# A chunked scan in pairs of 64-token chunks, and the old states' products in four column groups

## The chip, the cores and the metric

The kernel runs on one core of one Trainium2 chip. The metric is the device time of one launch in microseconds (us), median of three runs. The core's engines are TensorE (PE in the profile; PEld is its weight load), VectorE (DVE), ScalarE (ACT), GpSimd (POOL) and SyncE (SP), which issues the loads of the weights.

## The reference

One layer of a decoder with width 2048 is applied to a prompt of 256 tokens, with 16 learned meta tokens ahead of it, and to a sample group of 8 sequences of 4 tokens, which carry old states. All is float32. The input is normalised and projected. Half of the mixing width goes to eight heads of a gated linear recurrence, the other half to a short convolution. An output projection, a norm, a SwiGLU feed-forward part and a second norm follow. The change touches the recurrence alone:

```python
def step(S, inp):                       # one chunk of c tokens, per head
    qc, kc, vc, gc = inp
    b = jnp.cumsum(gc, axis=2)          # log of the decay since the chunk's start
    b_mid = b[:, :, mid:mid + 1]
    b_last = b[:, :, -1:]
    a = jnp.einsum('bhtk,bhsk->bhts', qc * jnp.exp(b - b_mid), kc * jnp.exp(b_mid - b))
    a = jnp.where(causal, a, 0.0)
    o = (jnp.einsum('bhts,bhsv->bhtv', a, vc)
         + jnp.einsum('bhtk,bhkv->bhtv', qc * jnp.exp(b), S))
    S = (jnp.exp(b_last[:, :, 0, :, None]) * S
         + jnp.einsum('bhsk,bhsv->bhkv', kc * jnp.exp(b_last - b), vc))
    return S, o
```

For the prompt the meta tokens are one chunk of 16 and the 256 tokens four chunks of 64. For the samples each sequence is one chunk of 4 tokens, and its S is the old state of that sequence and head, a matrix of 128 by 128. Results are the outputs of both groups, the new states and the convolution's last inputs.

## The kernel before, in words

Everything is kept feature-major: 128 features on the partitions, the 304 tokens (16 meta, 256 prompt, 32 sample) along the row. The weights come as a stream of pieces of 512 KB, each split into a high and a low part, `hi` (ScalarE, L72) and `lo` (VectorE, L73). A *job* (`run_job`, L161 on) makes two output blocks of 128 features from 16 blocks of input: for each input block six wide products, `hi` by the input's high part (L176), `hi` by its low part (L177), `lo` by its high part (L178). So a job of the input projection has 96 wide products. The order of the jobs is fixed by `ORDER`: four jobs for each pair of heads (`zb` the forget gate, `vb` the values, `qb`, `gb`), three for each pair of convolution blocks (`cb`, `xb`, `gbb`), 28 in all, and then those of `wo`, the output projection, 8 of them, and the feed-forward part.

Other work is written as generators that are laid beside the jobs. After each six wide products `tick()` lets every lane of generators go on by one step; `yield n` skips n such steps. The lane `scan` holds `scan_head`, one generator per head, one head after the other. A scheduler sets the order on each engine from there; each engine then works its list off in that order, and waits where an operand is not there.

A head (`scan_head`, L467 on) goes through these steps, each line a step or two of the lane. The bank names are those of the profile; each bank is 512 columns of f32 in PSUM, and four are cycled for this work (the wide products have four others).

- `vtb` (L480 to L482): transposes of the values to token-major: the two chunk pairs of the prompt, the samples, the meta tokens; `vsb` (L495): the sample values once more, four times over in high and low parts.
- On ScalarE and VectorE: the log forget gates, their running sums `b` (L521, started anew at each chunk), decays `eb`, `el` (L525 to L537), the queries and keys with decay `eq`, `ek`, `qe` (L550 to L554). GpSimd multiplies the old states by their decay, `sn` (L548).
- `ktb` (L559 to L561): transposes of the decayed keys; `ab` (L566, L567): keys by queries. Two prompt products of 128 tokens each hold two chunks; a mask (`cmask`, L576) keeps the causal part inside each chunk and writes it into `at_b`. The samples' 32 by 32 product goes through `smask` into `ats_b` (L577).
- `kv` (L583, L584): each chunk's addition to the state, from the 64 rows of that chunk; the two halves of a 128-row tile write to two banks. The meta tokens' is a product of 16 rows.
- `sb` (L587, L588): the samples' additions to all eight states. VectorE then makes the states ahead of chunks 0 to 3 (`sts`, L591, L595) and the last one (`sfin`), and adds `sb` to `sn` (L599, L601).
- `ob`: the outputs. For the prompt `at_b` by the values (L608), and for each chunk the state ahead of it by its queries, 64 columns each (L609). After one more step the samples: `ats_b` by the values (L611), and eight products of an old state by the four queries of its sequence (L614).
- `nb` (L621): the mean square of the outputs; then the norm, the gate and the split into `mh`, `ml`, which `wo` reads.

An f32 product stands in the profile as two instructions (two passes), each with its own weight load; the products of split operands and the transposes are one.

Of the kernel before, what the change touches and what calls it, by code (L numbers as in the profile page):

```python
# [45 lines left out]
class InOrder:  # L46
    """An engine whose instructions keep the order in which they are written."""
# [10 lines left out]
def hybrid_step(ctx: ExitStack, tc: tile.TileContext, io):  # L58
# [102 lines left out]
    def run_job(rhs, n, name):  # L161
        """Next job of the stream: two output blocks of 128 features, [P, n] each."""
        first, ks = jobs[state["job"]]
        nk = len(ks)
        state["job"] += 1
        banks = [bank(f"{name}{m}", "main") for m in range(2)]
        for i, k in enumerate(ks):
            p = first + i // KB
            if i % KB == 0:
                ensure(p)  # L170
            hi, lo = splits[p]
            xh, xl = rhs(k)
            for m in range(2):
                cs = slice(m * P, (m + 1) * P)
                o = banks[m][:, :n]
                nc.tensor.matmul(o, hi[:, i % KB, cs], xh, start=(i == 0), stop=False)  # L176
                nc.tensor.matmul(o, hi[:, i % KB, cs], xl, start=False, stop=False)  # L177
                nc.tensor.matmul(o, lo[:, i % KB, cs], xh, start=False, stop=(i == nk - 1))  # L178
            tick()
        for p in range(first, first + (nk + KB - 1) // KB):  # L180
            del splits[p]
        return banks

# [30 lines left out]
    smask = const.tile([NS, DB, DS], F32, name="smask")  # L214
# [6 lines left out]
    ats_b = const.tile([NS, DB, DS], F32, name="ats_b")  # L221
# [6 lines left out]
    def make_constants():  # L228
        nc.gpsimd.memset(cmask, 1.0)
        nc.gpsimd.affine_select(out=cmask, in_=cmask, compare_op=ALU.is_ge, fill=0.0, base=0,  # L230
                                pattern=[[0, NPR], [1, P]], channel_multiplier=-1)
        nc.gpsimd.memset(cmask[:CH, :, CH:], 0.0)
        nc.gpsimd.memset(smask, 1.0)
        nc.gpsimd.affine_select(out=smask, in_=smask, compare_op=ALU.is_ge, fill=0.0, base=0,
                                pattern=[[DS, DB], [1, DS]], channel_multiplier=-1)
        nc.gpsimd.affine_select(out=smask, in_=smask, compare_op=ALU.is_ge, fill=0.0, base=0,
                                pattern=[[-DS, DB], [0, DS]], channel_multiplier=1)
# [40 lines left out]
    def newton(r, v, t):  # L278
        """One step towards r = v ** -0.5."""
# [5 lines left out]
    def rstd_tok(pool, mv, n, w, tag):  # L285
        """mv [., w, 2] mean and variance per row -> 1/sqrt(variance + eps), -mean/sqrt(variance + eps)."""
# [17 lines left out]
    with tc.tile_pool(name="x0", bufs=1) as x0p, tc.tile_pool(name="x0w", bufs=3) as x0w:  # L304
# [29 lines left out]
        def rstd(i):  # L334
            """1/sqrt(variance + eps) and -mean/sqrt(variance + eps) of each row."""
# [39 lines left out]
        def settle(k):  # L375
            """Block k of the normalised input, feature-major."""
# [76 lines left out]
    sp = s2.enter_context(tc.tile_pool(name="sp", bufs=1))  # L453

# [6 lines left out]
    def sview(t, o=NMETA + SEQ):  # L461
        return t[:, o : o + NS].rearrange("p (c t) -> p c t", t=DS)
# [3 lines left out]

    def scan_head(h, j, zs, vs, qs, gs):  # L467
# [9 lines left out]
        # values, token-major; log forget gate, key  # L477
# [3 lines left out]
        nc.tensor.transpose(vtb[:NS, 2 * P : 3 * P], vT[:, NMETA + SEQ :], ident)  # L481
# [20 lines left out]
        vts = sp.tile([NS, P], F32, tag="vts", name="vts")  # L502
        nc.scalar.copy(out=vts, in_=vtb[:NS, 2 * P : 3 * P])
        vtm = sp.tile([NMETA, P], F32, tag="vtm", name="vtm")
        nc.scalar.copy(out=vtm, in_=vtb[:NMETA, 3 * P :])
# [8 lines left out]
        nc.scalar.activation(out=w2, in_=w2, func=AF.Ln, bias=1.0)  # L514
        yield 1
# [7 lines left out]
        # decay factors  # L523
# [11 lines left out]
        nc.vector.tensor_tensor(out=sview(tm, SEQ), in0=bs, in1=bs[:, :, DS // 2 : DS // 2 + 1].broadcast_to([P, DB, DS]), op=ALU.subtract)  # L535
        yield 1
        nc.vector.tensor_mul(out=el, in0=kk, in1=el)  # L537
# [13 lines left out]
        nc.vector.tensor_mul(out=ek, in0=kk[:, NMETA:], in1=ek)  # L551
        yield 1
        qe = tl("qe", L)
        nc.vector.tensor_mul(out=qe, in0=q, in1=eb)  # L554
        yield 1
        # decayed keys, token-major; products within chunks
        ktb = bank("ktb")
        for c in range(NPR):
            nc.tensor.transpose(ktb[:, c * P : (c + 1) * P], el[:, NMETA + c * P : NMETA + (c + 1) * P], ident)  # L559
        nc.tensor.transpose(ktb[:, 2 * P : 3 * P], kd4.rearrange("p a b -> p (a b)").bitcast(F32), ident)  # L560
        nc.tensor.transpose(ktb[:NMETA, 3 * P :], el[:, :NMETA], ident)  # L561
        yield 1
# [4 lines left out]
        nc.tensor.matmul(ab[:NS, SEQ:L], ek[:, SEQ:], eq[:, SEQ:], start=True, stop=True)  # L567
        yield 3
# [4 lines left out]
        kdm = sp.tile([NMETA, P], F32, tag="kdm", name="kdm")  # L573
        nc.scalar.copy(out=kdm, in_=ktb[:NMETA, 3 * P :])
        yield 1
        nc.vector.copy_predicated(out=at_b, mask=cmask.bitcast(I32), data=ab[:, :SEQ].rearrange("p (a b) -> p a b", b=P))  # L576
        nc.vector.copy_predicated(out=ats_b, mask=smask.bitcast(I32), data=ab[:NS, SEQ:L].rearrange("p (a b) -> p a b", b=DS))  # L577
        yield 1
        # each chunk's addition to the state
        kv = [bank("kv0"), bank("kv1")]  # L580
        for c in range(NCH):
            ts = slice(c % 2 * CH, c % 2 * CH + CH)
            nc.tensor.matmul(kv[c % 2][:, c // 2 * P : c // 2 * P + P], kdt[ts, c // 2], vt[ts, c // 2], start=True, stop=True)  # L583
        nc.tensor.matmul(kv[0][:, 2 * P : 3 * P], kdm, vtm, start=True, stop=True)  # L584
# [5 lines left out]
        sts = sp.tile([P, NCH, P], F32, tag="sts", name="sts")  # L590
        nc.vector.tensor_copy(out=sts[:, 0], in_=kv[0][:, 2 * P : 3 * P])  # L591
        sfin = sp.tile([P, P], F32, tag="sfin", name="sfin", bufs=2)
        for c in range(NCH):
            dst = sts[:, c + 1] if c < NCH - 1 else sfin
            nc.vector.scalar_tensor_tensor(out=dst, in0=sts[:, c], scalar=eb[:, c * CH + CH - 1 : c * CH + CH],  # L595
                                           in1=kv[c % 2][:, c // 2 * P : c // 2 * P + P], op0=ALU.mult, op1=ALU.add)
# [8 lines left out]
        for c in range(NCH):  # L605
            cs = slice(c * CH, (c + 1) * CH)
            if c % 2 == 0:
                nc.tensor.matmul(ob[:, c * CH : c * CH + P], vt[:, c // 2], at_b[:, c // 2], start=True, stop=False)  # L608
            nc.tensor.matmul(ob[:, cs], sts[:, c], qe[:, cs], start=False, stop=(c % 2 == 1))  # L609
        yield 1  # L610
        nc.tensor.matmul(ob[:, SEQ:L], vts, ats_b.rearrange("p a b -> p (a b)"), start=True, stop=False)  # L611
        for bb in range(DB):
            cs = slice(SEQ + bb * DS, SEQ + (bb + 1) * DS)
            nc.tensor.matmul(ob[:, cs], s0[:, bb], qe[:, cs], start=False, stop=(bb == DB - 1))  # L614
        yield LAG
        # norm over the value width, output gate
# [221 lines left out]
    def normed(bk, t, u):  # L838
        """t = the product of the normalised input, but for u[:, 1] = its bias' part."""
# [139 lines left out]
    def shared(i, c):  # L979
        """Chunk c of tile i on ScalarE and GpSimd."""  # L980
# [13 lines left out]
    def whole(i, c):  # L994
        """Chunk c of tile i on VectorE."""
# [5 lines left out]
    def packed():  # L1001
        """The last tokens' scale, and their chunk on VectorE."""
# [52 lines left out]
```

## Time and profile before

| What | Before |
|---|---|
| median of three runs | 1451.89 us |
| lowest and highest | 1451.75, 1455.24 us |
| profiled execution: first to last instruction | 1451.5 us |
| profiled execution: its own device time | not listed apart |
| mean granted clock of TensorE | 0.986 |
| instructions | 25280, of which 10389 products |
| HBM traffic over the span | 159 GB/s |

The scan's products run from 88 us (first `vtb`) to 453 us (last `nb`). The page lists busy time, share of the span and number for each engine; in its second part each digit is one fortieth of the span, the row PEclk being the clock that TensorE was granted, in tenths. In rows of groups the two numbers behind the bar are the busy time in us and the mean in ns. The busy time of a product covers its way through the array, in which the next ones already run; what a product costs is read from the distance of the starts.

### The profile page before, as it was taken

Reading aid. Unit: us, or ns where it says so; the run is one execution under the profiler, and the core shown is the slowest. Engines: PE = TensorE matmul, PEld = TensorE weight load, DVE = VectorE, ACT = ScalarE, POOL = GpSimd, SP = SyncE. Lnnn points to the kernel's source line nnn. Section 1 sums busy time; section 2 is a strip of 40 time slices with the busy share of each in tenths; the row PEclk is TensorE's granted clock in tenths of the full one; section 3 lists DMA queues with packets and bytes.
Section 4 is the critical chain, followed back from the end, with each engine's and each line's share of the span. In section 5 each row is a group of like instructions: output and inputs, shape, how many; then the busy total and the mean of one; then the engine's idle time right before and its main releaser. Section 6 shows DMA issues by size and latency. Waiting matters only on the chain.

```text
span 1451.5 us, 25280 instructions
## 1 busy us (share of the span) xinstructions
PE 1405.6 (97%) x10389; PEld 1389.5 (96%) x10389; DVE 880.1 (61%) x1526; ACT 591.9 (41%) x824; POOL 128.1 (9%) x165
## 2 busy tenths in 40 slices
PE   5999999999999999999999999999999999999993
PEld 4999999999999999999999999999999999999992
DVE  6756675776576778965565554444555656544444
ACT  5644534544443444433343333333333343343331
POOL 5201111121010233000000000000000000020002
PEclk9999999999999999999999999999999999999997
DMA  6645545544544555455555545555555555575521
GB/s 188 211 153 163 161 148 162 162 145 147 171 136 147 158 165 160 148 171 162 161 167 167 161 151 169 160 170 178 160 168 166 160 164 162 169 231 160 161 89 65
DMA packets 221065, 232.14 MB, mean 160 GB/s; under 512 B 7655, under 2 KB 216659, under 8 KB 220629
## 3 DMA queue, kind: packets, MB, share of 16 engines
q1 hardware_dynamic: 217556, 218.80, 47.9%
q0 software_dynamic: 3392, 11.72, 2.8%
q8 instruction: 81, 1.33, 0.4%
q14 instruction: 36, 0.29, 0.1%
HBM read 223.34 MB, written 7.15 MB: 159 GB/s over the span
## 4 chain that ended last, share of the span: by engine, by line
PE 95%; DVE 3%; DMA 0%; ACT 0%; issue 0%; POOL 0%; SPq 0%; ACTq 0%; DVEq 0%
PE u L176 7%; PE u L178 6%; PE u L177 6%; PE wd L178 6%; PE g L176 6%; PE wd L177 6%; PE g L178 6%; PE g L177 6%; PE wd L176 6%; PE wo L178 2%; PE wo L177 2%; PE wo L176 2%; PE zb L176 1%; PE vb L176 1%; PE zb L177 1%; PE gbb L176 1%
## 5 line engine op out<-in xcount | busy, mean ns | idle before, releaser
L73 DVE TENSOR_TENSOR lo<-raw,hi 128x1024 fp32r<-128x1024 f32 (+1 forms) x408 | 498.9, 1224 | 466.4 <-ACT hi L72 466.0
L72 ACT CAST hi<-raw 128x1024 fp32r<-128x1024 f32 (+1 forms) x408 | 420.5, 1031 | 648.0 <-PE wd L177 146.2
L176 PE MATMUL g<-ygh,hi 128*128 128x290 f32 x704 | 209.8, 298 | 0.0
L178 PE MATMUL g<-ygh,lo 128*128 128x290 f32 x704 | 209.3, 297 | 0.0
L177 PE MATMUL g<-ygl,hi 128*128 128x290 f32 x704 | 209.1, 297 | 0.0
L176 PE MATMUL u<-ygh,hi 128*128 128x290 f32 x704 | 208.8, 297 | 0.0
L178 PE MATMUL u<-ygh,lo 128*128 128x290 f32 x704 | 208.7, 296 | 0.0
L177 PE MATMUL u<-ygl,hi 128*128 128x290 f32 x704 | 208.5, 296 | 0.0
L178 PE MATMUL wd<-ah,lo 128*128 128x288 f32 x704 | 207.9, 295 | 0.0
L177 PE MATMUL wd<-al,hi 128*128 128x288 f32 x704 | 207.9, 295 | 0.0
L176 PE MATMUL wd<-ah,hi 128*128 128x288 f32 x704 | 207.7, 295 | 0.0
L177 PEld LDWEIGHTS g<-ygl,hi 128*128 128x128 f32 x704 | 133.9, 190 | 0.1
L178 PEld LDWEIGHTS g<-ygh,lo 128*128 128x128 f32 x704 | 133.7, 190 | 0.0
L176 PEld LDWEIGHTS g<-ygh,hi 128*128 128x128 f32 x704 | 133.6, 190 | 0.1
L177 PEld LDWEIGHTS u<-ygl,hi 128*128 128x128 f32 x704 | 133.2, 189 | 0.0
L178 PEld LDWEIGHTS u<-ygh,lo 128*128 128x128 f32 x704 | 133.2, 189 | 0.0
L176 PEld LDWEIGHTS u<-ygh,hi 128*128 128x128 f32 x704 | 133.0, 189 | 0.0
L177 PEld LDWEIGHTS wd<-al,hi 128*128 128x128 f32 x704 | 132.3, 188 | 0.0
L176 PEld LDWEIGHTS wd<-ah,hi 128*128 128x128 f32 x704 | 132.2, 188 | 0.1
L178 PEld LDWEIGHTS wd<-ah,lo 128*128 128x128 f32 x704 | 132.2, 188 | 0.0
L178 PE MATMUL wo<-mh,lo 128*128 128x288 f32 x256 | 75.8, 296 | 0.0
L177 PE MATMUL wo<-ml,hi 128*128 128x288 f32 x256 | 75.6, 295 | 0.0
(337 smaller groups left out, 2525.8 us busy)
## 6 DMA issues: line engine op xcount, KB each, us to landing
raw<-in_w_in SPq DMA_DIRECT2D x112, 512.0 KB, 3.5
raw<-in_w_gate SPq DMA_DIRECT2D x88, 512.0 KB, 3.4
raw<-in_w_up SPq DMA_DIRECT2D x88, 512.0 KB, 3.4
raw<-in_w_down SPq DMA_DIRECT2D x80, 512.0 KB, 3.5
raw<-in_w_o SPq DMA_DIRECT2D x32, 512.0 KB, 3.5
s<-in_state_hgrn POOLq DMA_DIRECT2D x8, 512.0 KB, 4.8
out<-sn POOLq DMA_DIRECT2D x8, 512.0 KB, 4.1
raw<-in_w_down SPq DMA_DIRECT2D x16, 256.0 KB, 2.8
```

The source lines that it names most:

```text
L72: a.copy(out=hi, in_=src)
L73: v.tensor_tensor(out=lo, in0=src, in1=hi.bitcast(F32), op=ALU.subtract)
L176: nc.tensor.matmul(o, hi[:, i % KB, cs], xh, start=(i == 0), stop=False)
L177: nc.tensor.matmul(o, hi[:, i % KB, cs], xl, start=False, stop=False)
L178: nc.tensor.matmul(o, lo[:, i % KB, cs], xh, start=False, stop=(i == nk - 1))
```

## The change

The prompt is scanned in two pairs of chunks instead of four chunks. For a pair, `kp` holds the keys with decay to their own chunk's end, and those of the first chunk once more with the decay over the second; `qp` holds the queries with decay from their chunk's start, for the second chunk also from the pair's start. `ktb` transposes keys with decay to the pair's end, so that `kv` is one product of 128 rows per pair, in one bank; `ep` is the decay over a pair, and VectorE makes two states instead of four. What the second chunk of a pair takes from the first one is an own product, keys of the first by queries of the second (`ab`, two products of 64 columns), and is copied into the upper right quarter of `at_b`. Each pair's output is then one product of 128 columns with the state ahead of the pair.

The meta tokens' operands `kdm` and `vtm` are zeroed tiles of 128 rows, of which 16 are written. The samples' values come from `vsb`, on 128 rows (high parts on rows 0 to 31 and 64 to 95, low parts on the others); the samples' keys stand four times (`ek4`), and `smask` keeps the rows 0 to 63, so that high and low parts add up.

The eight products of the old states become four, `so`: the 32 queries of all sequences are the weights, two old states side by side are moved (256 columns), and each product writes its own 32 partitions of one bank. VectorE picks from the two halves the rows that belong to the sequence (`pmask`, one column for each half) and adds them (`os`), and a product with `fold` adds the four groups of 32 rows and turns them to feature-major, into `ob`. The constants `pmask` and `fold` are made by GpSimd at the start. Of the steps, there are now three ahead of `ktb` instead of one, two ahead of `ab`, two ahead of `so` and one behind it, one behind `os`, and the one between the parts of `ob` is gone.

```diff
-    smask = const.tile([NS, DB, DS], F32, name="smask")
+    smask = const.tile([P, DB, DS], F32, name="smask")
+    pmask = const.tile([P, 2], F32, name="pmask")
+    fold = const.tile([P, NS], F32, name="fold")
...
+    kdm = sp.tile([P, P], F32, name="kdm")
+    vtm = sp.tile([P, P], F32, name="vtm")
+    nc.gpsimd.memset(kdm, 0.0)
+    nc.gpsimd.memset(vtm, 0.0)
...
-        nc.tensor.transpose(vtb[:NS, 2 * P : 3 * P], vT[:, NMETA + SEQ :], ident)
...
-        vts = sp.tile([NS, P], F32, tag="vts", name="vts")
-        nc.scalar.copy(out=vts, in_=vtb[:NS, 2 * P : 3 * P])
+        vts = sp.tile([P, P], F32, tag="vts", name="vts")
+        nc.scalar.copy(out=vts, in_=vsb[:, :P])
...
+        ends = pairs(eb[:, :SEQ])[:, :, :, CH - 1 : CH]
         yield 1
-        nc.vector.tensor_mul(out=el, in0=kk, in1=el)
+        kp = sp.tile([P, NPR, 3, CH], F32, tag="kp", name="kp")
+        nc.vector.tensor_mul(out=kp[:, :, 0::2], in0=pairs(kk[:, NMETA : NMETA + SEQ]), in1=pairs(el[:, NMETA : NMETA + SEQ]))
+        nc.vector.tensor_mul(out=el[:, NMETA + SEQ :], in0=kk[:, NMETA + SEQ :], in1=el[:, NMETA + SEQ :])
+        nc.vector.tensor_mul(out=el[:, :NMETA], in0=kk[:, :NMETA], in1=el[:, :NMETA])
+        nc.vector.tensor_tensor(out=kp[:, :, 1], in0=kp[:, :, 0], in1=ends[:, :, 1].broadcast_to([P, NPR, CH]), op=ALU.mult)
...
-        nc.vector.tensor_mul(out=ek, in0=kk[:, NMETA:], in1=ek)
-        yield 1
-        qe = tl("qe", L)
-        nc.vector.tensor_mul(out=qe, in0=q, in1=eb)
-        yield 1
+        nc.vector.tensor_mul(out=ek[:, :SEQ], in0=kk[:, NMETA : NMETA + SEQ], in1=ek[:, :SEQ])
+        ek4 = sp.tile([P, P // NS, NS], F32, tag="ek4", name="ek4")
+        nc.vector.tensor_tensor(out=ek4, in0=kk[:, NMETA + SEQ :].unsqueeze(1).broadcast_to([P, P // NS, NS]),
+                                in1=ek[:, SEQ:].unsqueeze(1).broadcast_to([P, P // NS, NS]), op=ALU.mult)
+        yield 1
+        qp = sp.tile([P, NPR, 3, CH], F32, tag="qp", name="qp")
+        nc.vector.tensor_mul(out=qp[:, :, 0::2], in0=pairs(q[:, :SEQ]), in1=pairs(eb[:, :SEQ]))
+        qe = sp.tile([P, NS], F32, tag="qe", name="qe")
+        nc.vector.tensor_mul(out=qe, in0=q[:, SEQ:], in1=eb[:, SEQ:])
+        nc.vector.tensor_tensor(out=qp[:, :, 1], in0=qp[:, :, 2], in1=ends[:, :, 0].broadcast_to([P, NPR, CH]), op=ALU.mult)
+        ep = sp.tile([P, NPR, 1], F32, tag="ep", name="ep")
+        nc.vector.tensor_mul(out=ep, in0=ends[:, :, 0], in1=ends[:, :, 1])
+        yield 3
...
-        nc.tensor.matmul(ab[:NS, SEQ:L], ek[:, SEQ:], eq[:, SEQ:], start=True, stop=True)
-        yield 3
+        nc.tensor.matmul(ab[:, SEQ:L], ek4.rearrange("p a b -> p (a b)"), eq[:, SEQ:], start=True, stop=True)
+        xs = slice(SEQ + CH, SEQ + CH + NPR * CH)
+        for c in range(NPR):
+            nc.tensor.matmul(ab[:, xs][:, c * CH : (c + 1) * CH], kp[:, c, 0:2].rearrange("p a b -> p (a b)"), qp[:, c, 2], start=True, stop=True)
+        yield 2
+        so = bank("so")
+        for g in range(P // NS):
+            nc.tensor.matmul(so[g * NS : (g + 1) * NS, : 2 * P], qe, s0[:, 2 * g : 2 * g + 2].rearrange("p a b -> p (a b)"),
+                             start=True, stop=True)
+        yield 1
...
+        nc.vector.tensor_copy(out=at_b[:CH, :, CH:], in_=ab[:CH, xs].rearrange("p (a b) -> p a b", b=CH))
+        nc.vector.copy_predicated(out=ats_b, mask=smask.bitcast(I32), data=ab[:, SEQ:L].rearrange("p (a b) -> p a b", b=DS))
+        yield 1
+        os_ = sp.tile([P, P], F32, tag="os", name="os")
+        nc.vector.tensor_scalar(out=os_, in0=so[:, :P], scalar1=pmask[:, 0:1], scalar2=None, op0=ALU.mult)
+        nc.vector.scalar_tensor_tensor(out=os_, in0=so[:, P : 2 * P], scalar=pmask[:, 1:2], in1=os_, op0=ALU.mult, op1=ALU.add)
         yield 1
-        kv = [bank("kv0"), bank("kv1")]
-        for c in range(NCH):
-            ts = slice(c % 2 * CH, c % 2 * CH + CH)
-            nc.tensor.matmul(kv[c % 2][:, c // 2 * P : c // 2 * P + P], kdt[ts, c // 2], vt[ts, c // 2], start=True, stop=True)
-        nc.tensor.matmul(kv[0][:, 2 * P : 3 * P], kdm, vtm, start=True, stop=True)
+        kv = bank("kv")
+        for c in range(NPR):
+            nc.tensor.matmul(kv[:, c * P : (c + 1) * P], kdt[:, c], vt[:, c], start=True, stop=True)
+        nc.tensor.matmul(kv[:, 2 * P : 3 * P], kdm, vtm, start=True, stop=True)
...
-        for c in range(NCH):
-            cs = slice(c * CH, (c + 1) * CH)
-            if c % 2 == 0:
-                nc.tensor.matmul(ob[:, c * CH : c * CH + P], vt[:, c // 2], at_b[:, c // 2], start=True, stop=False)
-            nc.tensor.matmul(ob[:, cs], sts[:, c], qe[:, cs], start=False, stop=(c % 2 == 1))
-        yield 1
+        for c in range(NPR):
+            cs = slice(c * P, (c + 1) * P)
+            nc.tensor.matmul(ob[:, cs], vt[:, c], at_b[:, c], start=True, stop=False)
+            nc.tensor.matmul(ob[:, cs], sts[:, c], qp[:, c, 0:2].rearrange("p a b -> p (a b)"), start=False, stop=True)
         nc.tensor.matmul(ob[:, SEQ:L], vts, ats_b.rearrange("p a b -> p (a b)"), start=True, stop=False)
-        for bb in range(DB):
-            cs = slice(SEQ + bb * DS, SEQ + (bb + 1) * DS)
-            nc.tensor.matmul(ob[:, cs], s0[:, bb], qe[:, cs], start=False, stop=(bb == DB - 1))
+        nc.tensor.matmul(ob[:, SEQ:L], os_, fold, start=False, stop=True)
```

The change also moves instructions. On TensorE, at the outputs of the first head, this is the order before (operation, out and in, partitions by columns of the result; numbers behind names are buffers):

```order
L608 MATMUL ob<-at_b,vt 128x128
L609 MATMUL ob<-qe,sts 128x64 x2
L608 MATMUL ob<-at_b,vt 128x128
L609 MATMUL ob<-qe,sts 128x64 x2
L176 MATMUL vb_1105<-xh,hi 128x304
L177 MATMUL vb_1105<-xl,hi 128x304
L178 MATMUL vb_1105<-xh,lo 128x304
L176 MATMUL vb_1106<-xh,hi 128x304
L177 MATMUL vb_1106<-xl,hi 128x304
L178 MATMUL vb_1106<-xh,lo 128x304
L611 MATMUL ob<-ats_b,vts 128x32
L614 MATMUL ob<-qe,s_968 128x4 x8
```

And this is the same place now:

```order
L650 MATMUL ob<-at_b,vt 128x128
L651 MATMUL ob<-qp,sts 128x128
L650 MATMUL ob<-at_b,vt 128x128
L651 MATMUL ob<-qp,sts 128x128
L652 MATMUL ob<-ats_b,vts 128x32
L653 MATMUL ob<-fold,os 128x32
```

Fifteen products in two blocks became six in one; the old states are read earlier, in a block of their own between `ab` and `kv`. On VectorE, in the third head, these are the instructions around the decayed keys that `ktb` transposes (`el` and `kd`; `up`, `us`, `y` belong to the convolution):

```order
L535 TENSOR_TENSOR w_1993<-b 128x32
L554 TENSOR_TENSOR qe<-q,eb 128x288
L646 TENSOR_TENSOR up<-xb_1809,cc 128x258
L73 TENSOR_TENSOR lo<-raw,hi 128x1024
L537 TENSOR_TENSOR el<-k,el 128x304
L550 TENSOR_TENSOR eq<-q,eq 128x288
L544 CAST kd_2015<-el 128x64
L551 TENSOR_TENSOR ek<-k,ek 128x288
L545 TENSOR_TENSOR kd_2015<-el,kd_2015 128x64
```

Now, from the first product of keys on (`kp`, `el`, `kd` are read by `ktb`):

```order
L556 TENSOR_TENSOR kp<-k,el 128x2x2x64
L557 TENSOR_TENSOR el<-k,el 128x32
L558 TENSOR_TENSOR el<-k,el 128x16
L559 TENSOR_TENSOR kp<-kp,eb 128x2x64
L566 CAST kd_2109<-el 128x64
L572 TENSOR_TENSOR eq<-q,eq 128x288
L567 TENSOR_TENSOR kd_2109<-el,kd_2109 128x64
L573 TENSOR_TENSOR ek<-k,ek 128x256
L575 TENSOR_TENSOR ek_2122<-k,ek 128x128
```

One product of 304 columns is four smaller ones, and neither the queries `qe` nor a `lo` stands between it and the keys' low parts any more; six instructions of the convolution (`y`) stand ahead of it that stood behind it.

More of the change, by code (lines that the diff above doesn't have):

```diff
@@ L220, in hybrid_step @@
     at_b = const.tile([P, NPR, P], F32, name="at_b")
-    ats_b = const.tile([NS, DB, DS], F32, name="ats_b")
+    ats_b = const.tile([P, DB, DS], F32, name="ats_b")
     bufT = const.tile([P, H, DB, 2], F32, name="bufT")
@@ L232, in make_constants @@
         nc.gpsimd.memset(cmask[:CH, :, CH:], 0.0)
[L233 to L237, printed above, removed]
+        nc.gpsimd.memset(smask, 0.0)
+        nc.gpsimd.memset(smask[: 2 * NS], 1.0)
+        for q in range(2):
+            sm = smask[q * NS : (q + 1) * NS]
+            nc.gpsimd.affine_select(out=sm, in_=sm, compare_op=ALU.is_ge, fill=0.0, base=0,
+                                    pattern=[[DS, DB], [1, DS]], channel_multiplier=-1)
+            nc.gpsimd.affine_select(out=sm, in_=sm, compare_op=ALU.is_ge, fill=0.0, base=0,
+                                    pattern=[[-DS, DB], [0, DS]], channel_multiplier=1)
         nc.gpsimd.memset(bmask, 1.0)
@@ L244, in make_constants @@
                                     pattern=[[DS, DB]], channel_multiplier=-1)
+            nc.gpsimd.tensor_copy(out=pmask[q * NS : (q + 1) * NS], in_=bm[:, 2 * q : 2 * q + 2])
+        nc.gpsimd.memset(fold, 0.0)
+        for q in range(P // NS):
+            nc.gpsimd.affine_select(out=fold, in_=fold, compare_op=ALU.not_equal, fill=1.0, base=-q * NS,
+                                    pattern=[[-1, NS]], channel_multiplier=1)
         nc.gpsimd.memset(reset, 1.0)
@@ L465, in lview, with pairs @@
         return t[:, :SEQ].rearrange("p (c t) -> p c t", t=CH)
+    def pairs(t):
+        return t.rearrange("p (a c t) -> p a c t", c=2, t=CH)
     def scan_head(h, j, zs, vs, qs, gs):
@@ L501, in scan_head @@
         nc.vector.tensor_copy(out=vt, in_=vtb[:, :SEQ].rearrange("p (a b) -> p a b", b=P))
-        vts = sp.tile([NS, P], F32, tag="vts", name="vts")
-        nc.scalar.copy(out=vts, in_=vtb[:NS, 2 * P : 3 * P])
-        vtm = sp.tile([NMETA, P], F32, tag="vtm", name="vtm")
-        nc.scalar.copy(out=vtm, in_=vtb[:NMETA, 3 * P :])
+        nc.scalar.copy(out=vtm[:NMETA], in_=vtb[:NMETA, 3 * P :])
         w2 = tl("w2")
@@ L572, in scan_head @@
         nc.scalar.copy(out=k4t, in_=ktb[:, 2 * P : 3 * P])
[L573 to L574 removed]
+        nc.scalar.copy(out=kdm[:NMETA], in_=ktb[:NMETA, 3 * P :])
         yield 1
         nc.vector.copy_predicated(out=at_b, mask=cmask.bitcast(I32), data=ab[:, :SEQ].rearrange("p (a b) -> p a b", b=P))
[L577 removed]
+        nc.vector.tensor_copy(out=at_b[:CH, :, CH:], in_=ab[:CH, xs].rearrange("p (a b) -> p a b", b=CH))
+        nc.vector.copy_predicated(out=ats_b, mask=smask.bitcast(I32), data=ab[:, SEQ:L].rearrange("p (a b) -> p a b", b=DS))
         yield 1
[L580 to L584 removed]
+        os_ = sp.tile([P, P], F32, tag="os", name="os")
[6 more added lines that the diff above has]
+        nc.tensor.matmul(kv[:, 2 * P : 3 * P], kdm, vtm, start=True, stop=True)
         yield 1
@@ L589, in scan_head @@
         yield 3
-        sts = sp.tile([P, NCH, P], F32, tag="sts", name="sts")
-        nc.vector.tensor_copy(out=sts[:, 0], in_=kv[0][:, 2 * P : 3 * P])
+        sts = sp.tile([P, NPR, P], F32, tag="sts", name="sts")
+        nc.vector.tensor_copy(out=sts[:, 0], in_=kv[:, 2 * P : 3 * P])
         sfin = sp.tile([P, P], F32, tag="sfin", name="sfin", bufs=2)
-        for c in range(NCH):
-            dst = sts[:, c + 1] if c < NCH - 1 else sfin
-            nc.vector.scalar_tensor_tensor(out=dst, in0=sts[:, c], scalar=eb[:, c * CH + CH - 1 : c * CH + CH],
-                                           in1=kv[c % 2][:, c // 2 * P : c // 2 * P + P], op0=ALU.mult, op1=ALU.add)
+        for c in range(NPR):
+            dst = sts[:, c + 1] if c < NPR - 1 else sfin
+            nc.vector.scalar_tensor_tensor(out=dst, in0=sts[:, c], scalar=ep[:, c], in1=kv[:, c * P : (c + 1) * P],
+                                           op0=ALU.mult, op1=ALU.add)
         nc.gpsimd.dma_start(out=io["out_2"][0, 0, h], in_=sfin)
```

5 lines of the change are left out of this document (3 added, 2 removed).

## The prediction, on record before the run

> **What bounds the kernel now.** I read the page first: busy shares, the clock row, the chain that ended last.
>
> ```profile
> PE 1405.6 (97%) x10389; PEld 1389.5 (96%) x10389; DVE 880.1 (61%) x1526; ACT 591.9 (41%) x824; POOL 128.1 (9%) x165
> PEclk9999999999999999999999999999999999999997
> PE 95%; DVE 3%; DMA 0%; ACT 0%; issue 0%; POOL 0%; SPq 0%; ACTq 0%; DVEq 0%
> ```
>
> TensorE is busy nearly throughout, and 95% of the chain is its own instructions: a microsecond of TensorE time taken out anywhere shortens the run by that, unless something else then makes TensorE wait. All heads of the scan run between 40 and 480 us, beside the input products. So I went to the timeline of PE for one head. The columns are start, duration, engine, line, operation. Durations overlap, since products are pipelined; the cost of a block is the distance between starts, less the pitch of the wide products (0.13 to 0.14 us).
>
> ```profile
> 113.04 0.30 PE L178 MATMUL vb<-xh,lo 128*128 128x304 f32 x1
> 113.18 0.38 PE L608 MATMUL ob<-at_b,vt 128*128 128x128 f32 x2
> ...
> 114.07 0.56 PE L609 MATMUL ob<-qe,sts 128*128 128x64 f32 x4
> 114.43 0.39 PE L176 MATMUL vb<-xh,hi 128*128 128x304 f32 x1
> 114.66 0.30 PE L177 MATMUL vb<-xl,hi 128*128 128x304 f32 x1
> ...
> 115.21 0.30 PE L178 MATMUL vb<-xh,lo 128*128 128x304 f32 x1
> 115.44 0.40 PE L611 MATMUL ob<-ats_b,vts 32*128 32x32 f32 x2
> 115.77 1.95 PE L614 MATMUL ob<-qe,s 128*128 128x4 f32 x16
> 117.58 0.38 PE L176 MATMUL qb<-xh,hi 128*128 128x288 f32 x1
> 117.80 0.30 PE L177 MATMUL qb<-xl,hi 128*128 128x288 f32 x1
> ```
>
> Each f32 product is two passes. The sixteen passes of the old states (L614) take 117.58 - 115.77 = 1.81 us, 0.113 us each, though each moves 4 columns only; the passes of 64 and 128 columns cost the same (12 in about 1.34 us). Up to 128 columns the price of a pass is thus a constant 0.113. The first part of `ob` costs 114.66 - 113.04 - 0.28 = 1.34 us, the second 117.80 - 115.21 - 0.27 = 2.32.
>
> **The change, part by part: TensorE.** The other two blocks that change:
>
> ```profile
> 100.52 0.30 PE L178 MATMUL vb<-xh,lo 128*128 128x304 f32 x1
> 100.66 0.60 PE L566 MATMUL ab<-eq,ek 128*128 128x128 f32 x4
> 101.19 0.25 PE L567 MATMUL ab<-eq,ek 128*32 128x32 f32 x2
> 101.37 0.41 PE L176 MATMUL vb<-xh,hi 128*128 128x304 f32 x1
> 101.62 0.30 PE L177 MATMUL vb<-xl,hi 128*128 128x304 f32 x1
> ...
> 105.49 0.30 PE L178 MATMUL vb<-xh,lo 128*128 128x304 f32 x1
> 105.72 0.71 PE L583 MATMUL kv<-vt,kdt 64*128 64x128 f32 x8
> 106.36 0.48 PE L584 MATMUL kv<-vtm,kdm 16*128 16x128 f32 x2
> 106.77 0.41 PE L176 MATMUL vb<-xh,hi 128*128 128x304 f32 x1
> 107.02 0.30 PE L177 MATMUL vb<-xl,hi 128*128 128x304 f32 x1
> ```
>
> `ab` costs 101.62 - 100.52 - 0.28 = 0.82, `kv` 107.02 - 105.49 - 0.28 = 1.25. Eight 64-row passes of `kv` fit between 105.72 and 106.36, 0.08 each, below the 0.113: two row groups run at once. What is won there goes to the joints around the 16-row product. The smaller form has a joint in `ab` too: 0.82 less four passes (0.45) leaves 0.37 for two 32-column passes, which I split into 0.10 for them and 0.27 for changing form and back.
>
> Before, a head pays 1.34 + 2.32 + 0.82 + 1.25 + 0.11 (the transpose of the sample values that goes) = 5.84 us. After: `ab` ten passes of at most 128 columns, 1.13; `kv` six full-height passes, 0.68; `ob` twelve passes, 1.36, all in the common form, without joints: 3.17. New is `so`: four products of 32 output partitions, 256 columns, eight passes. Wide f32 passes are priced by the norm:
>
> ```profile
> 122.43 0.65 PE L621 MATMUL nb<-w,ones_h 128*128 128x288 f32 x2
> ...
> 123.05 0.29 PE L177 MATMUL qb<-xl,hi 128*128 128x288 f32 x1
> ```
>
> (123.05 - 122.43 - 0.13) / 2 = 0.243 per pass of 288 columns, so 0.216 for 256. No row shows column groups side by side. One after another the eight cost 1.73; two at a time, as the row groups of `kv` do, 0.86; all four at a time 0.43. With the joint of 0.27: 2.00, 1.13 or 0.70. I take 1.13, as `kv` is the nearest row. A head then gains 5.84 - 3.17 - 1.13 = 1.54, eight heads **12.3 us** (ends 5.3 and 15.7). The Trainium skill (TensorE: Matmul & The Clock Gate, Part 3) gives 2.38 times for three column tiles; scaled to four, `so` would be an estimated 0.54 + 0.27 = 0.81, and the gain 14.9. The same part has small-K products run concurrently in row tiles, which speaks against padding `kv` to full height: the trace agrees on the 0.08 per pass, but by its rows the padded six passes still cost 0.57 less, as the joints go.
>
> **Waits and the clock.** TensorE waits for VectorE in this stage, in two heads, at the transposes of the decayed keys:
>
> ```profile
> 182.74 0.44 PE L559 MATMUL ktb<-ident,el 128*128 128x128 f32 x2 [1.81 <-DVE el L537]
> 428.22 0.33 PE L560 MATMUL ktb<-ident,kd 128*128 128x128 f32 x1 [0.86 <-DVE kd L545]
> ```
>
> And the clock falls to half in four places. I cut windows there; the number behind the engines is PEclk:
>
> ```profile
> 184.06:187.47 3.41, 3.41 (x16) 3.12 (x16) 3.41 (x11) 0.68 (x3) 1.56 (x4) 0.50 0.32 112
> 289.87:293.28 3.41, 3.41 (x30) 3.20 (x28) 2.00 (x6) 1.05 (x1) 0.18 (x1) 1.00 0.60 180
> 293.28:300.11 6.83, 6.83 (x31) 6.83 (x31) 3.21 (x11) 0.50 (x2) 1.73 (x5) 0.50 0.53 156
> 446.88:450.30 3.42, 3.42 (x17) 3.42 (x16) 0.00 (x0) 0.79 (x1) 0.00 (x0) 0.50 0.00 1
> 112.38:115.79 3.41, 3.41 (x28) 3.19 (x27) 0.65 (x1) 0.66 (x2) 0.00 (x0) 1.00 0.91 264
> ```
>
> The half-clock stretches are 3.41 or 6.83 us long, and their starts lie whole multiples of 3.413 apart (from 184.06 to 293.28 109.22, which is 32 of them; on to 446.88 153.60, 45 of them): a fixed grid. A fourth, of 3.41 us, lies between the last two shown. The first follows the wait at 182.74. The other three follow a grid window that holds both parts of an `ob`, 30 instructions of which the sixteen moved next to nothing. At 113 the same two parts fell on either side of a grid line (115.79), and the clock stayed at 1.00. So I read them as windows with too little streaming. At half clock wide products start 0.24 us apart instead of 0.134:
>
> ```profile
> 186.04 0.44 PE L178 MATMUL gbb<-xh,lo 128*128 128x288 f32 x1
> 186.28 0.44 PE L176 MATMUL gbb<-xh,hi 128*128 128x288 f32 x1
> ```
>
> So 44% is lost, of 17.07 us **7.5**. The change takes the sixteen 4-column passes away; of the new blocks `ob` has eight full passes of twelve, and `so` streams 256 columns. I forecast all four stretches gone (ends: none gone, 0; all gone and also the one at the later norm, 9).
>
> The Trainium skill (TensorE: Matmul & The Clock Gate, Part 1) ties the half clock to idle windows of 3.4 us on a free-running grid. The trace agrees on length and grid, not on idleness: PE is listed busy 3.41 of 3.41 us before the second stretch. If only idleness counted, the clock term would not come from the small products; that is the second rival.
>
> The waits: both have VectorE late with the decayed keys. In the order of TensorE's instructions 72 wide products now stand between the transpose into `vsb` and this block, where 60 stood (the longer `yield` ahead of `ktb`), 1.6 us more at 0.134. VectorE has to do more ahead of it: the product of 304 columns becomes four (256, 32, 16 and 128 columns).
>
> ```profile
> sum 440.00, PE 437.33 PEld 427.75 DVE 287.27 ACT 204.91 POOL 56.18; mean PE 48.59 PEld 47.53 DVE 31.92 ACT 22.77 POOL 6.24
> L595 DVE SCALAR_TENSOR_TENSOR sts<-sts,eb,kv 128x128 f32<-128x128 f32 x24 | 8.3, 345 | 0.4
> L537 DVE TENSOR_TENSOR el<-k,el 128x304 f32<-128x304 f32 x8 | 3.8, 471 | 0.2
> L576 DVE COPY_PREDICATED at_b<-cmask,ab 128x256 f32<-128x256 int32 x8 | 3.6, 446 | 7.0 <-PE ab L567 7.0
> L535 DVE TENSOR_TENSOR w<-b x8: 179/184/1910, 61.5 to 423.7; 128x32 f32<-128x32 f32 x8
> ```
>
> By these (L535's numbers are the least, the median and the most of eight, in ns), 0.45 + 0.18 + 0.18 + 0.35 - 0.47 = 0.69 us more ahead of `ktb`, against 1.6 us more room: of the 1.81 and 0.86 I count both gone, **2.7 us** (ends 0 and 2.7). Over a head VectorE gains thirteen instructions (three of 256 columns, three of 128 for keys and queries, the copy into `at_b`, two of `so`, four of 32 or less: 3 x 0.45 + 6 x 0.35 + 4 x 0.18 = 4.2) and loses five (the 304-column one and two of 288, 1.4 at the 0.47 of L537, two of L595, 0.7): +2 us, 16 in all, on an engine busy 287 of 440 us. That lies beside TensorE; without that room it would cost up to 2 us a head. What stands behind a late instruction on VectorE is the weights' low parts, and behind those the wide products. ScalarE keeps its copies (the sample values come from the other bank, still one). GpSimd's extra masks go into the 8.55 us in which it waits at the start:
>
> ```profile
> 18.55 3.02 POOL L128 TENSOR_TENSOR lo<-raw,hi 128x256 fp32r<-128x256 f32 x4 [8.55 <-ACT hi L54]
> ```
>
> About a dozen of them at a few tenths, some 3 us: nothing on the path; without that cover, up to 3. The DMAs are the same.
>
> Sum: 12.3 + 7.5 + 2.7 = 22.5. The profiled span is 1451.5, so 1429.0; the median of the runs lies 0.4 above the span: **1429.4 us**. Its own range, from the ends for `so` and 2 us either way for the clock, is 1424 to 1434.
>
> **The rivals.** (1) Column groups run one after another: `so` costs 2.00 and the gain in instructions is 5.3, so 1451.9 - 5.3 - 10.2 = 1436.4. For it: no row shows column groups overlapping, and the four write one bank, where `kv` alternates between two. Against: `kv` overlaps. (2) The clock falls as often as before: other blocks sit on grid lines, or streaming was not the cause; 1451.9 - 15.0 = 1436.9. For it: the phase of the grid is chance. Against: the window at 112.38. With (1) as well, 1443.9. (3) VectorE becomes the bound at the transposes: it is late in every head by the 1.81 us seen once, and each such wait brings one half-clock stretch (3.41 x 0.44 = 1.5): 8 x 3.3 = 26.4, against 10.2 that these cost now and 12.3 gained, so 3.9 slower, 1455.8. It decides from 2.8 us a head (22.5 / 8). For it: eight instructions more on balance, and a 32-column one (L535 above) takes ten times its median in one head; such a hold-up can come again. Against: 1.6 us more room, and 35% of VectorE's time idle. (4) The gain is lost in joints and new waits, and no difference shows.
>
> **How the numbers follow.** Forecast 55%, (1) 15%, (2) 16%, both 6%, (3) 4%, (4) 4%. The range reaches over (1) and (2): 1420 to 1441 leaves out both together, (3), (4) and a little of each end. A measurement here tells 0.3% (4.4 us) from no change, so faster 0.92, same 0.04, slower 0.04.
>
> **What would show it.** `so`: eight passes in 0.7 to 1.3 us of starts; 1.7 or more is rival (1). `kv` about 0.7, `ob` one block of about 1.4. No PEclk of 0.50 between 100 and 460 us; each one left costs 1.5 us. No wait above 0.5 us at `ktb`, `ab`, `so` or `kv`; one for VectorE in most heads would be rival (3) and make the forecast wrong, as would a scan that is not shorter by at least 10 us up to the start of `wo`.

## The result

The changed kernel takes **1428.09 us** (median of 4 runs, 1427.02 to 1429.04), against 1453.57 us for the kernel before (4 runs, 1451.75 to 1456.58). The ratio is 0.9819, with a 95% interval of 0.9806 to 0.9832. The profiled execution has a span of 1426.9 us, 24.6 less than the one before.

The page of the changed kernel, with the lines that answer to those shown of before:

```profile
PE 1384.3 (97%) x10301; PEld 1369.8 (96%) x10301; DVE 887.2 (62%) x1590; ACT 593.4 (42%) x824; POOL 124.3 (9%) x179
PEclk9999999999999999999999999999999999999996
```

TensorE is still the bound; its listed busy time, which takes in what a halved clock stretched, is 21 us shorter. VectorE has 7 us more, beside it. The same windows of both kernels, first before, then after (length, busy time of PE, PEld, DVE, ACT, POOL with numbers of instructions, granted clock, DMA share, GB/s):

```profile
27.05:31.90 4.85, 4.85 (x33) 4.15 (x31) 3.41 (x6) 3.45 (x6) 2.45 (x3) 1.00 0.29 99
88.00:460.00 372.00, 369.33 (x2701) 360.40 (x2700) 243.59 (x453) 167.27 (x283) 48.09 (x52) 0.98 0.50 153
```

```profile
27.05:31.90 4.85, 4.85 (x19) 3.92 (x18) 3.38 (x6) 3.00 (x5) 2.70 (x3) 1.00 0.21 73
88.00:460.00 372.00, 372.00 (x2813) 364.97 (x2812) 266.12 (x537) 179.87 (x300) 42.91 (x54) 1.00 0.55 165
...
31.90:1404.00 1372.10, 1368.09 (x10243) 1357.21 (x10242) 853.69 (x1518) 573.96 (x792) 96.36 (x113) 1.00 0.53 163
```

In the scan's stretch the clock is 1.00 throughout, where it was 0.98 with four drops; it stays at 1.00 up to 1404 us, the later norm included. The list of TensorE's waits has no row for `ktb` any more. At the start, though, 19 products ran where 33 had run: there the changed kernel lost 1.9 us, (33 - 19) x 0.134. The clock's own record has it rise at 31.9 us, not at 27.05 (the mean of a window before the first rise reads 1.00, as nothing is recorded there).

The whole gain stands where the change was made: the first product of `wo` starts at 441.62 us, where it was 466.29 before, 24.7 earlier. From there to the end both take the same time (985.3 and 985.2 us).

The blocks of the first head, on the timeline of PE (start, duration, engine, line):

```profile
104.80 0.30 PE L178 MATMUL vb<-xh,lo 128*128 128x304 f32 x1
104.94 0.60 PE L597 MATMUL ab<-eq,ek 128*128 128x128 f32 x4
105.39 0.31 PE L598 MATMUL ab<-eq,ek 128*128 128x32 f32 x2
105.53 0.64 PE L601 MATMUL ab<-qp,kp 128*128 128x64 f32 x4
105.97 0.39 PE L176 MATMUL vb<-xh,hi 128*128 128x304 f32 x1
106.20 0.30 PE L177 MATMUL vb<-xl,hi 128*128 128x304 f32 x1
...
107.59 0.30 PE L178 MATMUL vb<-xh,lo 128*128 128x304 f32 x1
107.82 0.64 PE L606 MATMUL so<-s,qe 128*32 128x256 f32 x8
108.39 0.41 PE L176 MATMUL vb<-xh,hi 128*128 128x304 f32 x1
108.64 0.30 PE L177 MATMUL vb<-xl,hi 128*128 128x304 f32 x1
...
111.69 0.30 PE L178 MATMUL vb<-xh,lo 128*128 128x304 f32 x1
111.83 0.60 PE L626 MATMUL kv<-vt,kdt 128*128 128x128 f32 x4
...
112.64 0.30 PE L177 MATMUL vb<-xl,hi 128*128 128x304 f32 x1
...
118.54 0.29 PE L178 MATMUL qb<-xh,lo 128*128 128x288 f32 x1
118.67 0.38 PE L650 MATMUL ob<-at_b,vt 128*128 128x128 f32 x2
...
119.70 0.39 PE L653 MATMUL ob<-fold,os 128*128 128x32 f32 x2
...
120.14 0.29 PE L177 MATMUL qb<-xl,hi 128*128 128x288 f32 x1
```

By the distances, less two pitches of 0.135 to 0.14: `ab` 1.12 us, `so` 0.77, `kv` 0.67, `ob` 1.33. All eight passes of `so`, 256 columns each, begin and end within 0.64 us. The other heads agree within 0.02 us, those of the kernel before too where the clock is not halved.

| Per head, us | before | forecast | after |
|---|---|---|---|
| `ab` | 0.82 | 1.13 | 1.12 |
| `so` | none | 1.13 (0.70 to 2.00) | 0.77 |
| `kv` | 1.25 | 0.68 | 0.67 |
| `ob` | 3.66 | 1.36 | 1.33 |
| one transpose | 0.11 | none | none |
| sum | 5.84 | 4.30 | 3.89 |

### The profile page after: what moved, and what is told of

Same layout as the page of the kernel before. It is cut to its first block, busy times and chain, and to the rows that moved or that the text cites. A ratio compares the mean times of both kernels' runs of the same rounds, so it can differ in the third digit from the quotient of the medians.

```text
span 1426.9 us, 25210 instructions
## 1 busy us (share of the span) xinstructions
PE 1384.3 (97%) x10301; PEld 1369.8 (96%) x10301; DVE 887.2 (62%) x1590; ACT 593.4 (42%) x824; POOL 124.3 (9%) x179
## 3 DMA queue, kind: packets, MB, share of 16 engines
q8 instruction: 81, 1.33, 0.4%
## 4 chain that ended last, share of the span: by engine, by line
PE 96%; DVE 2%; DMA 0%; POOL 0%; issue 0%; ACT 0%; SPq 0%; ACTq 0%; DVEq 0%
PE u L176 7%; PE u L177 7%; PE u L178 7%; PE g L176 7%; PE wd L178 7%; PE wd L177 7%; PE g L177 7%; PE wd L176 7%; PE g L178 7%; PE wo L178 2%; PE wo L177 2%; PE wo L176 2%; PE zb L176 2%; PE zb L177 1%; PE zb L178 1%; PE vb L176 1%
```

## The experiments

The theory under test is that of the prediction: the blocks add up from passes, joints and column groups that run side by side; the clock is halved after a grid window in which too little is streamed; the two extra steps ahead of `ktb` take the waits away.

**Only the old states' products are changed** (`old_states_only`; the kernel before, with `so`, `os` and `fold`):

```diff
         nc.tensor.matmul(ab[:NS, SEQ:L], ek[:, SEQ:], eq[:, SEQ:], start=True, stop=True)
-        yield 3
+        yield 2
+        so = bank("so")
+        for g in range(P // NS):
+            nc.tensor.matmul(so[g * NS : (g + 1) * NS, : 2 * P], qe[:, SEQ:], ...)
+        yield 1
...
-        for bb in range(DB):
-            cs = slice(SEQ + bb * DS, SEQ + (bb + 1) * DS)
-            nc.tensor.matmul(ob[:, cs], s0[:, bb], qe[:, cs], start=False, stop=(bb == DB - 1))
+        nc.tensor.matmul(ob[:, SEQ:L], os_, fold, start=False, stop=True)
```

> The kernel before with the old states' products alone changed: four column-group products `so` behind `ab`, picked by the mask and folded; chunks of 64, `kv` and the meta tokens' product as before. Theory (prices of passes and joints add up, and windows with little streaming halve the clock): the second part of `ob` falls from 2.32 us to about 0.75 (the 32-row product with its joint, and two passes of `fold`), `so` costs 0.77, so 0.8 us a head and 6.4 us in all; the three half-clock stretches behind `ob` (four grid windows, 1.5 us each) go, the wait at `ktb` and its stretch stay: about 12 us faster than before, PEclk 0.50 at most behind `ktb`. Rival (the clock falls for waits alone, or by the phase): 6 us faster, with stretches behind `ob` still there.

Measured: 1443.22 us, 0.9934 of before (0.9917 to 0.9951), some 9 us faster and not 12. The timeline at the samples' part of `ob`, the waits at `ktb` (total, times, longest), and the one window of half clock in the scan:

```profile
117.95 0.30 PE L178 MATMUL vb<-xh,lo 128*128 128x304 f32 x1
118.18 0.40 PE L626 MATMUL ob<-ats_b,vts 32*128 32x32 f32 x2
118.52 0.41 PE L627 MATMUL ob<-fold,os 128*128 128x32 f32 x2
118.76 0.38 PE L176 MATMUL qb<-xh,hi 128*128 128x288 f32 x1
118.98 0.29 PE L177 MATMUL qb<-xl,hi 128*128 128x288 f32 x1
```

```profile
PE ktb L567 <- DVE kd L552: 2.0, 2, 1.2
PE ktb L566 <- DVE el L544: 1.8, 1, 1.8
```

```profile
184.24:187.65 3.41, 3.41 (x16) 3.11 (x15) 3.41 (x11) 0.67 (x3) 1.75 (x4) 0.50 0.40 132
```

The block is 118.98 - 117.95 - 0.27 = 0.76 us, as expected, so the instruction part of 6.4 us is there. No stretch follows an `ob`; the one behind the wait stayed. The waits grew from 2.7 to 3.8 us, where I had counted them as unchanged: 1.1 us of the miss. The rest is what the grid decides. From the first `vtb` to the first product of `wo` this kernel takes 367.0 us, the first profile of the kernel before 378.3: 11.3 are gained there, the 12.4 of the sum (6.4 and four windows of 1.5) less those 1.1. But the clock rose later at the start (30.64 us, not 27.05), which took 2.0 back, and the second profile of the kernel before, with fewer half-clock windows (below), takes 376.0 for the scan, only 9.0 more.

**Only the pairs are changed** (`pairs_only`; the changed kernel without `so`, `os` and `fold`):

```diff
-        nc.tensor.matmul(ob[:, SEQ:L], os_, fold, start=False, stop=True)
+        for bb in range(DB):
+            cs = slice(SEQ + bb * DS, SEQ + (bb + 1) * DS)
+            nc.tensor.matmul(ob[:, cs], s0[:, bb], qe[:, bb * DS : (bb + 1) * DS], start=False, stop=(bb == DB - 1))
```

> The changed kernel with the old states' products as before: eight products of 4 columns in `ob`, no `so`, no mask, no fold; the scan stays in pairs. Theory: against the changed kernel sixteen passes of 0.113 come in for `so` (0.77) and two passes of `fold` (0.22): 0.82 us a head, 6.6 us slower than the changed kernel, some 18 us faster than before, if the clock holds; each half-clock stretch that comes back adds 1.5 us. The block now has eight full passes beside eighteen short ones, so I expect fewer stretches than the four of before, 0 to 2. Rival (most of the gain came from the old states): less than 10 us faster than before.

Measured: 1434.52 us, 0.9879 of before (0.9861 to 0.9897): 17.5 us faster than before, 6.4 slower than the changed kernel's 1428.09. The timeline at `ob`, and the scan's window:

```profile
115.73 0.29 PE L178 MATMUL qb<-xh,lo 128*128 128x288 f32 x1
115.86 0.38 PE L642 MATMUL ob<-at_b,vt 128*128 128x128 f32 x2
...
116.89 1.93 PE L647 MATMUL ob<-qe,s 128*128 128x4 f32 x16
118.68 0.38 PE L176 MATMUL qb<-xh,hi 128*128 128x288 f32 x1
118.90 0.29 PE L177 MATMUL qb<-xl,hi 128*128 128x288 f32 x1
```

```profile
100.00:460.00 360.00, 359.98 (x2725) 357.63 (x2724) 248.86 (x501) 171.32 (x286) 42.84 (x52) 1.00 0.54 162
```

`ob` is 118.90 - 115.73 - 0.27 = 2.90 us: 1.57 more than in the changed kernel, less the 0.77 of `so`, gives 0.80 a head and 6.4 in all. The clock holds at 1.00 over the scan, though the sixteen short passes are all there (the one half-clock window of this profile is at the later norm, from 556.20 us). That was not the phase of the grid: in five of the eight heads all sixteen lie in one grid window. One of these windows runs from 327.51 to 330.92 us; here with the window behind it:

```profile
327.51:334.33 6.82, 6.82 (x57) 6.82 (x56) 1.65 (x3) 2.84 (x5) 0.89 (x1) 1.00 0.57 163
```

Besides the sixteen only one of the block's full-height passes starts in that window, and eleven wide products. The window from 336.54 us of the kernel before (`before_again`, below), which is followed by half clock, has the sixteen, the 32-row product with its joint, and eight wide products. So I read the difference by the joint that is gone and the wide products that take its place; that reading was not tested.

**The column groups one after another** (`one_group`; all four `so` products write partitions 0 to 31, so the samples' outputs lack the old states' part):

```diff
-            nc.tensor.matmul(so[g * NS : (g + 1) * NS, : 2 * P], qe, ...)
+            nc.tensor.matmul(so[:NS, : 2 * P], qe, ...)
```

> The changed kernel, but the four `so` products all write the same 32 partitions, one after another over the same values, and four copies of that stand in for the two picks (the samples' outputs lack the old states' part). Theory (the four column groups run at the same time): eight passes of 0.216 and the joint make 2.0 us instead of 0.77, 1.2 us a head, 10 us slower than the changed kernel, about 15 faster than before. Rival (a pass of 32 output columns is cheap by itself): `so` stays below 1.1 us and the time is that of the changed kernel within 3 us.

Measured: 1438.87 us, 0.9909 of before (0.9892 to 0.9925). Its `so`:

```profile
106.22 0.30 PE L178 MATMUL vb<-xh,lo 128*128 128x304 f32 x1
106.45 1.91 PE L606 MATMUL so<-s,qe 128*32 128x256 f32 x8
108.29 0.41 PE L176 MATMUL vb<-xh,hi 128*128 128x304 f32 x1
108.54 0.30 PE L177 MATMUL vb<-xl,hi 128*128 128x304 f32 x1
```

108.54 - 106.22 - 0.28 = 2.04 us, against 0.77 with four groups. The difference of 1.27 us is 8 x 0.216 less a quarter of it (1.73 - 0.43 = 1.30): the groups run four at a time, and the joint is 0.3 us in both. The whole run is 10.8 us slower than the changed kernel's 1428.09; eight times 1.27 are 10.2.

**The old states' products made wide** (`old_states_wide`; the kernel before, each of the eight products moves 128 columns into a free part of the bank, so the samples' outputs lack the old states' part):

```diff
-            nc.tensor.matmul(ob[:, cs], s0[:, bb], qe[:, cs], start=False, stop=(bb == DB - 1))
+            nc.tensor.matmul(ob[:, L : L + P], s0[:, bb], qe[:, :P], start=(bb == 0), stop=(bb == DB - 1))
```

> The kernel before, but each of the eight products of an old state moves 128 columns of queries into a free part of the bank instead of 4 (the samples' outputs lack the old states' part). The passes should cost what they cost, 0.11 us, so the instruction time is unchanged. Theory (a grid window with too little streaming halves the clock): no half-clock stretch behind `ob`, at most the one behind the wait at `ktb`; 4.5 to 7.5 us faster than before. Rival (idleness or waits halve the clock, or the number of instructions): the stretches behind `ob` stay and the time is that of before within 2 us.

Measured: 1446.34 us, 0.9957 of before (0.994 to 0.9973), 5.7 us faster with the same number of instructions. Its sixteen passes (the timeline), and windows cut at the changes of the clock (the first takes in two heads' `ob`, the last six, and ends behind the scan):

```profile
117.48 2.05 PE L613 MATMUL ob<-qe,s 128*128 128x128 f32 x16
119.28 0.38 PE L176 MATMUL qb<-xh,hi 128*128 128x288 f32 x1
```

```profile
31.75:185.35 153.60, 151.80 (x1118) 147.34 (x1116) 98.94 (x169) 79.97 (x132) 21.62 (x19) 1.00 0.55 166
185.35:188.77 3.42, 3.42 (x17) 3.00 (x16) 3.42 (x12) 0.69 (x4) 1.80 (x4) 0.50 0.42 141
188.77:571.06 382.29, 380.69 (x2846) 373.72 (x2845) 268.34 (x451) 171.92 (x274) 63.81 (x72) 1.00 0.53 159
```

The passes cost the same 0.113 us ((119.28 - 117.48) / 16) with 32 times the columns, and no stretch follows an `ob`, although in the first and the fourth head all sixteen lie in one grid window (from 117.09 and 243.38 us). Nor is it one lucky profile: the granted clock of its six runs is 0.990 to 0.993, that of the eleven runs of the kernel before beside them 0.985 to 0.989. What halved the clock there is thus how little streams through the array in a grid window. The instructions themselves, and PE's listed busy time, do not differ. The stretch behind the wait at `ktb` is still there.

**The kernel before once more, for its clock** (`before_again`, no edit):

> The kernel before once more, for its clock. Theory (a free grid against fixed blocks): the stretch behind the wait at `ktb` in the third head or its neighbourhood again; the stretches behind `ob` in other heads or in another number, 1 to 5 grid windows in all. Rival (a fixed property of those three heads): behind the same three `ob`, at about 293, 403 and 447 us.

```profile
203.42:206.84 3.42, 3.42 (x16) 3.42 (x15) 0.98 (x1) 1.05 (x1) 0.34 (x1) 0.50 0.61 153
295.58:298.99 3.41, 3.41 (x15) 3.41 (x16) 2.73 (x11) 0.41 (x1) 1.73 (x5) 0.50 0.66 198
339.96:343.37 3.41, 3.41 (x16) 3.41 (x15) 0.00 (x0) 0.32 (x1) 0.46 (x1) 0.50 0.59 157
```

Measured: 1451.21 us, a single run. Its only three half-clock windows in the scan follow the `ob` of the third, the fifth and the sixth head; in the first profile it was the fifth, the seventh and the eighth. And this time none follows the wait of 1.8 us at `ktb`, which is there again, 0.24 us of it ahead of a grid line. So the grid is free, and the number of hits differs from one execution to the next: five windows in one profile, three in the other. That fits the runs of the kernel before lying 5 us apart, and those of the changed one 2. The listed clock of the 18 runs of the kernel before that stand beside the experiments is 0.985 to 0.989, in the middle 0.988; the first profile has 0.986, this one 0.989.

The starts on the timelines say how much of the block a window had to hold. In the two profiles each of the four full-clock windows with all sixteen short passes is followed by half clock, and the one with fifteen; of three with thirteen one is (289.87), and of those with twelve or fewer none. A window with thirteen that is not followed, from 334.25 to 337.66 us of the first profile, with the window behind it:

```profile
334.25:341.07 6.82, 6.82 (x54) 6.60 (x54) 1.23 (x1) 1.30 (x3) 0.90 (x1) 1.00 0.65 181
```

**The two steps ahead of `ktb` taken back** (`early_ktb`):

```diff
         nc.vector.tensor_mul(out=ep, in0=ends[:, :, 0], in1=ends[:, :, 1])
-        yield 3
+        yield 1
```

> The changed kernel with one step instead of three ahead of the transposes of the decayed keys (`ktb`), so that 60 wide products stand between `vsb` and `ktb` as before, not 72. Theory (the two steps are what took the waits for VectorE away): waits for VectorE at `ktb` come back in one to four heads, 2 to 6 us in all, and a half-clock stretch (1.5 us) may follow the longest: 2 to 7 us slower than the changed kernel. Rival (VectorE had room, the waits went because the work ahead of them is ordered otherwise): no wait above 0.5 us and the same time within 1.5 us.

Measured: 1434.31 us, 0.9877 of before (0.986 to 0.9895), 6.1 us slower than the changed kernel beside it (1428.24). Its waits:

```profile
PE ktb L590 <- DVE kp L559: 5.3, 4, 2.0
PE ktb L591 <- DVE kd L567: 0.3, 2, 0.2
```

Four heads wait, three of them for 1.4 to 2.0 us, where two waited before the change. That fits the longer work of VectorE ahead of `ktb`, which was not varied by itself. No half-clock window followed. The steps are worth 6 us here: without them a quarter of the gain would have gone to waits.

**The meta tokens' product with 16 rows** (`meta_16`):

```diff
-        nc.tensor.matmul(kv[:, 2 * P : 3 * P], kdm, vtm, start=True, stop=True)
+        nc.tensor.matmul(kv[:, 2 * P : 3 * P], kdm[:NMETA], vtm[:NMETA], start=True, stop=True)
```

> The changed kernel, but the meta tokens' product of `kv` takes 16 rows again instead of 128 zeroed ones. Theory (changing the form of the product drains the array, some 0.2 us at each side): `kv` rises from 0.67 to 0.9 to 1.1 us, 2 to 3.5 us in all. Rival (the joints of before belonged to the 64-row groups): `kv` stays at 0.67 and the time is the same.

Measured: 1431.14 us, 0.9848 of before (0.9834 to 0.9863), 2.9 us slower than the changed kernel beside it. Its `kv`:

```profile
110.69 0.30 PE L178 MATMUL vb<-xh,lo 128*128 128x304 f32 x1
110.83 0.60 PE L626 MATMUL kv<-vt,kdt 128*128 128x128 f32 x4
111.36 0.48 PE L627 MATMUL kv<-vtm,kdm 16*128 16x128 f32 x2
111.78 0.41 PE L176 MATMUL vb<-xh,hi 128*128 128x304 f32 x1
112.03 0.30 PE L177 MATMUL vb<-xl,hi 128*128 128x304 f32 x1
```

112.03 - 110.69 - 0.28 = 1.06 us against 0.67: two passes of fewer rows cost 0.39 us more than two full ones, all of it at the joints, 3.1 us in eight heads. The zeroed rows pay.

**The changed kernel once more** (`after_again`, no edit):

> The changed kernel once more, beside the two others. Theory: no half-clock stretch between 100 and 460 us again, `so` 0.77, `ob` 1.34, no wait at `ktb`; the moment at which the clock rises at the start (31.9 us in the first profile, 27.1 before) lies elsewhere, since the grid does not start with the kernel. Rival (the absence of the stretches was the luck of the grid): one or more of them.

Measured: 1428.24 us, 0.9828 of before (0.9814 to 0.9843). No half clock between 100 and 460 us again, nor in the profiles of the other four runs with the scan in pairs; `so` is 0.77 and `ob` 1.33 us again, and `ktb` has no wait. The rise at the start lies at 29.8 us in it, between the two others.

## Why the prediction was right, point by point

- **The bound.** TensorE's own time set the end before and sets it now; what was taken out there came out of the total.
- **Instructions.** The forecast was 12.3 us; measured are 5.84 - 3.89 = 1.95 us a head, 15.6 us. Passes at 0.113 us, `ab`, `kv` and `ob` came within 0.03 us a head. The mis-sized term is `so`: I took it as two groups at a time, by the two row groups of `kv`; all four column groups run at once, 0.77 us, close to the lower end. The figure for three column tiles in the Trainium skill (TensorE: Matmul & The Clock Gate, Part 3), scaled to four, had given an estimate of 0.81. Rival (1) fell, and `one_group` shows what it would have cost.
- **The padding of `kv`.** It was right by the rows: `kv` fell from 1.25 to 0.67 us. `meta_16` shows that the joint alone is worth 0.39 us a head.
- **The clock.** All four stretches in the scan went, as forecast; `old_states_wide` shows that little streaming made those behind `ob`. The reading of the windows was too coarse, though. That from 443.47 holds no first part of its `ob`, only the second; that from 334.25 holds parts of both, just as the one from 289.87, and was not followed. The forecast needed only that no window of the new kernel be so poor, and that held in every profile of the scan in pairs; rival (2) fell there. Counting one profile's windows was a step too short: the free grid gave five there and three in the next, so 7.5 us is the upper part of what the kernel before loses (three cost 4.5). Where the Trainium skill (TensorE: Matmul & The Clock Gate, Part 1) speaks of idle windows, the runs show that windows that PE is listed busy in can do it.
- **The norm.** That its half-clock window is missing from the changed kernel's profile is luck. The first profile of the kernel before has it, and so have those of `old_states_wide` and `pairs_only`; the other seven have not, `before_again` among them.
- **The waits.** Both went. `early_ktb` shows that the two steps did it, and that without them the waits would be 5.3 us, twice those of before; rival (3) named the mechanism, but the room was enough. On VectorE the forecast counted 16 us more; 7.1 are listed.
- **What I left out.** The changed kernel's profile lost 1.9 us at the start, as the clock rose later. The rise lies on the same grid (in the kernel before, 46 windows ahead of the first drop). In the ten profiles of this study it comes anywhere from 27.1 to 31.9 us; one window, 3.41, can be the phase, and the rest of the spread stays open.

The sum on the profiles goes by stretches. Up to the first `vtb` 1.9 us are lost. From there to `wo` the time fell from 378.3 to 351.8 us, by 26.5, of which 15.6 (instructions), 7.5 (clock) and 2.7 (waits) make 25.8. From `wo` on nothing is won, though the window at the norm (about 1.5 us) is gone: from the first product of `g` to the last of `wd`, in the feed-forward part, the changed kernel takes 855.0 us in both its profiles, where `before_again`, also without that window, takes 853.5. `old_states_only` takes 855.0 too; why the products lie a little further apart is not on record.

Part of the closeness is luck. The span was forecast as 1429.0 us and is 1426.9: `so` gave 3.3 us more than counted, the start took 1.9 back. To get the time, 0.4 us were added to the span, but each run listed with both has about 1.7 us between them; so the time came out nearer, 1.3 us off. And the upper end of the range, 1434, does not follow from what it is said to come from: `so` at 2.00 and 2 us of clock make 1438.4.

## What to carry to other kernels

A short f32 product of full height costs a constant price per pass, here 0.113 us from 4 to 128 columns: count passes, not arithmetic, and swap operands so that the wide one is moved. Products that use only 32 output partitions pay off when four of them follow one another on four column groups; a single product of another form pays for its joints (0.39 us in `kv`) and is better padded with zeros. Work that is moved onto another engine needs its steps moved with it, or part of the gain is lost to waits. And one profile is not enough to count what a free grid decides.

## What was not expected of the hardware

- The four column groups ran fully side by side with f32 operands into one bank: eight passes of 256 columns in 0.77 us with the joint, against 2.04 on one group.
- The clock was halved for a grid window of 3.41 us, once for two, after windows in which TensorE was never listed idle, and this went away when the same instructions moved 128 columns instead of 4. What a window had to hold was seen for this block alone (thirteen of the sixteen short passes or more); no general limit was measured, and waits of up to 2.0 us were not always followed.
- What that clock costs differs from one execution to the next: 1.9 us at the start between the two first profiles, and 4.5 or 7.5 us in the scan of the kernel before, by the phase of the grid.
